# A rotary embedding on one core: VectorE's program aligned to an instruction-fetch line, and ScalarE's copies by half rows

## The chip, the cores and the metric

The kernel runs on one core of one Trainium2 chip. The metric is the device time of one execution in microseconds (us). A core has TensorE (PE in the profile), VectorE (DVE), ScalarE (ACT), GpSimd (POOL) and SyncE (SP), which run their own programs and meet at semaphores, and 16 DMA engines between the memory of the chip (HBM) and the on-chip memory, where the tiles lie.

## The reference

The input x has 16 batches of 512 positions of 1,024 numbers (16 heads of 64). In each head the first 32 numbers are rotated against the last 32, by tables of cosines and sines that depend on the position. All is float32.

```python
x1, x2 = x[..., :half_dim], x[..., half_dim:]
rotated = np.concatenate([x1 * cos - x2 * sin, x1 * sin + x2 * cos], axis=-1)
```

So each number is multiplied by a cosine, and the number 32 places away in its head, multiplied by plus or minus the sine, is added. Input and output have 33.55 MB each.

## The kernel before, in words

Two batches make a tile of 128 partitions by 8 rows of 1,024 numbers (4 MiB); there are eight tiles, in five buffers. SyncE issues all transfers from one queue: the first tile in two parts with the sine and cosine tables between them, the next four tiles, four tiny reads into a spare buffer (L92), and then the stores, one per tile, but two of 2 MiB for the last. Loads of tiles 5 to 7 follow the third store (L78, L74).

Before the tiles, GpSimd writes an identity matrix. VectorE clears a tile of zeros (L97), with which TensorE opens its PSUM buffers (L101), and copies the identity twice beside itself (L109, `spread`). TensorE multiplies the tables by it (L113, L114), which lays them out over all partitions; VectorE writes signed sines from that (L116, L117, L119).

The eight rows of a tile are computed in three ways:

- Six rows, as three pairs (`PAIRS`): VectorE multiplies by the cosine into PSUM (L141, `pd`), GpSimd multiplies the swapped halves by the sine (L165, `b`), VectorE adds the two back into the tile (L189).
- Row 3 (`pe_half`), in two halves of 512: VectorE's cosine product goes into `pe_ps` (L141), GpSimd makes the sine product, TensorE adds it through the identity (L176), and ScalarE copies the sum back into the tile (L181).
- Row 0, the own row: VectorE multiplies by the cosine into `own_ps` (L141), then by the sine in place (L150). TensorE adds the swapped row to `own_ps` through the identity, 512 numbers at a time, which are the two halves of `own_ps` (L176), and ScalarE copies the sum back (L209).

The order of the work is written out by hand and stands in the loop over the tiles; nothing reorders it. The cosine product of the next tile's own row comes near the end of each tile's turn.

Of the kernel before, what the change touches and what calls it, by code (L numbers as in the profile page):

```python
# [28 lines left out]
def kernel(  # L29
# [13 lines left out]
    nc = tc.nc  # L43
# [20 lines left out]
    pd = ctx.enter_context(tc.tile_pool(name="pd", bufs=1, space=bass.MemoryType.PSUM))  # L64

    ctx.enter_context(tc.manual_schedule())

    tiles = [None] * NT

# [28 lines left out]
    own_ps = pe.tile([P, dim], FP32)  # L98
    pe_ps = pe.tile([P, BANK], FP32)
    for ps in (own_ps[:, :BANK], own_ps[:, BANK:], pe_ps):  # L100
# [9 lines left out]
        out=spread.rearrange("p (b q) -> p b q", b=NB),  # L110
        in_=bass.AP(tensor=eye.tensor, offset=eye.offset, ap=[eye.ap[0], [0, NB], [1, PB]]),
# [12 lines left out]
    def swapped(r):  # L124
        n = r.shape[1] // hd
        return bass.AP(tensor=r.tensor, offset=r.offset + half, ap=[r.ap[0], [hd, n], [-half, 2], [1, half]])

    def rows(t, k, n=1):
        return tiles[t][:, k * dim : (k + n) * dim]

    def cos_product(out, r, k, n=1):

        c = cos_t[:, k * half : (k + n) * half]
        m = r.shape[1] // (n * half)
        if n == 1:
            cb = bass.AP(tensor=c.tensor, offset=c.offset, ap=[c.ap[0], [0, m], [1, half]])
            o, i = (z.rearrange("p (a j) -> p a j", j=half) for z in (out, r))
        else:
            cb = bass.AP(tensor=c.tensor, offset=c.offset, ap=[c.ap[0], [half, n], [0, m], [1, half]])
            o, i = (z.rearrange("p (k a j) -> p k a j", k=n, j=half) for z in (out, r))  # L140
        nc.vector.tensor_tensor(out=o, in0=i, in1=cb, op=ALU.mult)  # L141

    def own_product(r):

        s = bass.AP(
            tensor=own_t.tensor,
            offset=own_t.offset + half,
            ap=[own_t.ap[0], [0, nh], [-half, 2], [1, half]],
        )
        nc.vector.tensor_tensor(out=heads(r), in0=heads(r), in1=s, op=ALU.mult)  # L150
# [16 lines left out]
    def sin_rows(t, k, n):  # L167
        b = bp.tile([P, 2 * dim], FP32, name="b")[:, : n * dim]
        sin_product(b, rows(t, k, n), k, n)
        return b  # L170

    def parts(r):
        return [r[:, i * BANK : (i + 1) * BANK] for i in range(r.shape[1] // BANK)]

    def pe_add(ps, other):
        nc.tensor.matmul(out=ps, lhsT=ident, rhs=other, start=False, stop=True, skip_group_check=True)  # L176

    def pe_half(k, r, b):
        cos_product(pe_ps, r, k)
        pe_add(pe_ps, b)  # L180
        nc.scalar.copy(out=r, in_=pe_ps)  # L181

    def pair_product(t, k):
        ps = pd.tile([P, 2 * dim], FP32, name="pd")
        cos_product(ps, rows(t, k, 2), k, 2)
        return ps, rows(t, k, 2)

    def pair_sum(ps, r, b):
        nc.vector.tensor_tensor(out=r, in0=ps, in1=b, op=ALU.add)  # L189

    def stores(t):
        lo = 0
        for hi in LAST_OUT if t == NT - 1 else (KK,):
            store(t, lo, hi)
            lo = hi
        if t + 1 == NT - BUFS:
            for n in range(BUFS, NT):
                load(n)

    cos_product(own_ps, rows(0, ROW_OWN), ROW_OWN)  # L200
    for t in range(NT):
        first, second, third = PAIRS
        b1 = sin_rows(t, first[0], 2)
        p1 = pair_product(t, first[0])
        r0 = rows(t, ROW_OWN)
        own_product(r0)
        for ps, r in zip(parts(own_ps), parts(r0)):
            pe_add(ps, swapped(r))
        nc.scalar.copy(out=r0, in_=own_ps)  # L209
        b3 = sin_rows(t, ROW_PE, 1)  # L210
        b2 = sin_rows(t, second[0], 2)
        pair_sum(*p1, b1)
        h0, h1 = zip(parts(rows(t, ROW_PE)), parts(b3))
        pe_half(ROW_PE, *h0)
        p2 = pair_product(t, second[0])
        b1 = sin_rows(t, third[0], 2)
        pair_sum(*p2, b2)
        pe_half(ROW_PE, *h1)
        p1 = pair_product(t, third[0])
        if t + 1 < NT:  # L220
            cos_product(own_ps, rows(t + 1, ROW_OWN), ROW_OWN)
        pair_sum(*p1, b1)
        stores(t)
# [35 lines left out]
```

## Time and profile before

| | |
|---|---|
| median of 7 runs | 162.65 us (162.2 to 162.82) |
| the profiled execution | 162.36 us |
| its span, first to last instruction | 160.6 us (160.57) |
| busy: VectorE, GpSimd, TensorE, ScalarE | 136.2, 127.2, 56.9, 18.7 us |
| DMA: data packets, share of 16 engines | 98.0% |
| DMA: instruction packets | 1 |

The span is what the profile draws; the rest of an execution's time lies before and after it. Busy times are sums over one engine's instructions. The DMA share is the time that packets took, out of 16 engines over the whole span. An instruction packet is a piece of an engine's program that is fetched while it runs. In lists of groups, a row names line, engine, operation, what it writes and reads, and how often; then its busy time, the mean of one in ns, and the idle time before it with what ended it. In the table of stretches, the columns are TensorE's matmuls and weight loads, VectorE, ScalarE and GpSimd with their busy time and number of instructions, then TensorE's granted clock, the DMA share and GB/s. In a timeline, the first two numbers are start and length.

### The profile page before, as it was taken

The page shows a single profiled execution, that of the slowest core. Times are in us where ns is not written, and L with a number is a line of the kernel's source. Part 1 is how long each engine was busy: PE and PEld are TensorE (multiplying, and loading weights), DVE is VectorE, ACT ScalarE, POOL GpSimd, SP SyncE. Part 2 cuts the span into 40 slices and gives each one's busy share as a digit, 9 for nine tenths or more (in the row PEclk, how much of TensorE's full clock was granted, in tenths as well). Part 3 has the DMA queues.
Part 4 walks back from the last instruction along what each step waited for, and adds up shares of the span by engine and source line. Part 5 has one row for each costly group of instructions (what it writes and reads, how often), then busy time and mean ns, then how long its engine had stood idle before and what let it go on. Part 6 is the DMA issues. An engine that isn't in the chain of part 4 may idle for free.

```text
span 160.6 us, 443 instructions
## 1 busy us (share of the span) xinstructions
PE 56.9 (35%) x71; PEld 18.3 (11%) x71; DVE 136.2 (85%) x85; ACT 18.7 (12%) x25; POOL 127.2 (79%) x38
## 2 busy tenths in 40 slices
PE   3041905057303930193108420672049201930000
PEld 0011201021002200130003000210022001300000
DVE  1059969999999999999999999999999999999000
ACT  0001411003100211012100310031002200211000
POOL 1039999999999999988998899898998899840000
PEclk9999975556855595558555765568555955585555
DMA  5999999999999999999999999999999999999994
GB/s 187 396 413 473 392 490 424 392 465 449 392 433 474 400 400 506 400 392 514 402 392 465 441 400 433 473 392 424 473 408 424 473 408 408 482 416 400 429 424 192
DMA packets 2787, 67.25 MB, mean 419 GB/s; under 512 B 354, under 2 KB 482, under 8 KB 482
## 3 DMA queue, kind: packets, MB, share of 16 engines
q1 hardware_dynamic: 2786, 67.24, 98.0%
q14 instruction: 1, 0.01, 0.0%
HBM read 33.69 MB, written 33.55 MB: 419 GB/s over the span
## 4 chain that ended last, share of the span: by engine, by line
DVE 68%; issue 12%; POOL 6%; DMA 4%; PE 1%; SPq 0%; DVEq 0%
DVE xt L189 33%; DVE pd L141 31%; POOL b L165 6%; DMA b<-in_sin_dram 4%; DVE pe_ps L141 3%; PE tab L113 1%; PE tab L114 1%; DVE sns L116 0%; DVE xt L150 0%; DVE own_ps L141 0%; SPq L74 0%; DVE sns L117 0%; DVEq L189 0%
## 5 line engine op out<-in xcount | busy, mean ns | idle before, releaser
L165 POOL TENSOR_TENSOR b<-xt,sns 128x2048 f32<-128x2048 f32 (+1 forms) x32 | 126.5, 3980 | 14.7 <-DVE sns L117 9.3
L189 DVE TENSOR_TENSOR xt<-pd,b 128x2048 f32<-128x2048 f32 x24 | 54.9, 2286 | 2.4 <-POOL b L165 1.6
L141 DVE TENSOR_TENSOR pd<-xt,tab 128x2048 f32<-128x2048 f32 x24 | 55.0, 2291 | 0.2
L176 PE MATMUL own_ps<-xt,ident 128*128 128x512 f32 x32 | 30.0, 1093 | 59.1 <-DVE xt L150 53.3
L176 PE MATMUL pe_ps<-b,ident 128*128 128x512 f32 x32 | 25.0, 874 | 22.7 <-DVE pe_ps L141 22.7
L176 PEld LDWEIGHTS own_ps<-xt,ident 128*128 128x128 f32 x32 | 9.4, 324 | 75.2 <-DVE xt L150 60.5
L209 ACT COPY xt<-own_ps 128x1024 f32<-128x1024 f32 x8 | 8.1, 1012 | 78.1 <-PE own_ps L176 78.1
L181 ACT COPY xt<-pe_ps 128x512 f32<-128x512 f32 x16 | 9.4, 586 | 33.2 <-PE pe_ps L176 33.2
L176 PEld LDWEIGHTS pe_ps<-b,ident 128*128 128x128 f32 x32 | 7.4, 253 | 43.0 <-DVE pe_ps L141 34.5
L141 DVE TENSOR_TENSOR pe_ps<-xt,tab 128x512 f32<-128x512 f32 x16 | 11.0, 686 | 0.0
L141 DVE TENSOR_TENSOR own_ps<-xt,tab 128x1024 f32<-128x1024 f32 x8 | 9.8, 1224 | 0.0
L150 DVE TENSOR_TENSOR xt<-xt,tab 128x1024 f32<-128x1024 f32 x8 | 9.7, 1214 | 0.0
L116 DVE TENSOR_SCALAR sns<-tab 128x256 f32<-128x256 f32 x1 | 0.4, 425 | 8.2 <-PE tab L114 8.2
L209 ACT ACT_TABLE_LOAD x1 | 1.3, 1283 | 15.4 <-DVE xt L150 15.4
L113 PE MATMUL tab<-b,spread 64*128 64x256 f32 x2 | 1.2, 696 | 5.0 <-DMA b<-in_sin_dram 5.0
L101 PE MATMUL own_ps<-zero 128*128 128x512 bf16 x2 | 1.0, 620 | 1.2 <-DVE zero L97 1.2
L113 PEld LDWEIGHTS tab<-b,spread 64*128 64x128 f32 x2 | 0.5, 307 | 5.9 <-issue 5.9
L114 PE MATMUL tab<-b,spread 64*128 64x256 f32 x2 | 1.1, 631 | 0.0
L97 DVE MEMSET zero<- 128x256 uint32 x1 | 0.3, 272 | 0.9 <-PEq L240 0.9
L114 PEld LDWEIGHTS tab<-b,spread 64*128 64x128 f32 x2 | 0.7, 333 | 0.2
L101 PE MATMUL pe_ps<-zero 128*128 128x512 bf16 x1 | 0.6, 634 | 0.0
L101 PEld LDWEIGHTS <-zero 128*128 128x128 bf16 x3 | 0.3, 123 | 1.5 <-DVE zero L97 1.2
(9 smaller groups left out, 1.8 us busy)
## 6 DMA issues: line engine op xcount, KB each, us to landing
xt<-in_x_dram SPq DMA_DIRECT2D x7, 4096.0 KB, 29.7
out_dram<-xt SPq DMA_DIRECT2D x7, 4096.0 KB, 24.7
out_dram<-xt SPq DMA_DIRECT2D x2, 2048.0 KB, 10.4
xt<-in_x_dram SPq DMA_DIRECT2D x1, 2560.0 KB
xt<-in_x_dram SPq DMA_DIRECT2D x1, 1536.0 KB
b<-in_sin_dram SPq DMA_DIRECT2D x1, 64.0 KB
b<-in_cos_dram SPq DMA_DIRECT2D x1, 64.0 KB
spare<-in_sin_dram SPq DMA_DIRECT2D x1, 0.1 KB
```

Of the source, the lines that this page charges most:

```text
L97: nc.vector.memset(zero, 0.0)
L101: nc.tensor.matmul(out=ps, lhsT=zero[:, :P], rhs=zero, start=True, stop=True)
L113: nc.tensor.matmul(out=sin_t, lhsT=spread, rhs=sin_sb, start=True, stop=True)
L114: nc.tensor.matmul(out=cos_t, lhsT=spread, rhs=cos_sb, start=True, stop=True)
L116: nc.vector.tensor_scalar_mul(out=sns[:, :, 0, :], in0=sin_k, scalar1=-1.0)
L141: nc.vector.tensor_tensor(out=o, in0=i, in1=cb, op=ALU.mult)
L150: nc.vector.tensor_tensor(out=heads(r), in0=heads(r), in1=s, op=ALU.mult)
L165: nc.gpsimd.tensor_tensor(out=o, in0=i, in1=sb, op=ALU.mult)
L176: nc.tensor.matmul(out=ps, lhsT=ident, rhs=other, start=False, stop=True, skip_group_check=True)
L181: nc.scalar.copy(out=r, in_=pe_ps)
L189: nc.vector.tensor_tensor(out=r, in0=ps, in1=b, op=ALU.add)
L209: nc.scalar.copy(out=r0, in_=own_ps)
```

## The change

```diff
     ctx.enter_context(tc.manual_schedule())
+    nc.vector.addr_align(128, max_nops=0)
...
         own_product(r0)
         for ps, r in zip(parts(own_ps), parts(r0)):
             pe_add(ps, swapped(r))
-        nc.scalar.copy(out=r0, in_=own_ps)
+            nc.scalar.copy(out=r, in_=ps)
```

The first line puts an alignment into VectorE's program, ahead of its first instruction of the kernel's body: what follows it begins at a multiple of 128 instruction slots, and VectorE gets there by a branch over the padding. The second moves ScalarE's copy of the own row into the loop over its halves. In the built program ScalarE has 16 copies of 512 numbers where there were eight of 1,024; TensorE's instructions are the same and in the same order, but the matmul of the second half waits for a semaphore of ScalarE that it didn't wait for before, and VectorE's cosine product into `own_ps` no longer waits for TensorE. ScalarE's program grows from 45 to 53 instructions; VectorE's goes from 125 to 122, with the alignment itself among them. GpSimd's and SyncE's are as they were.

## The prediction

> **What bounds the kernel now.** I read four views, in this order. First the page's slices, the DMA table and the chain of the work that ended last:
>
> ```profile
> span 160.6 us, 443 instructions
> ...
> DMA  5999999999999999999999999999999999999994
> ...
> q1 hardware_dynamic: 2786, 67.24, 98.0%
> q14 instruction: 1, 0.01, 0.0%
> ...
> DVE 68%; issue 12%; POOL 6%; DMA 4%; PE 1%; SPq 0%; DVEq 0%
> ```
>
> The chain blames VectorE (68%), but the 16 DMA engines are busy from the first slice to the last, and only one packet is not data: one instruction fetch. Two rows that can't both bind, so the second view is the table of stretches:
>
> ```profile
> 124.00:141.00 17.00, 6.64 (x9) 2.10 (x8) 16.86 (x11) 2.18 (x3) 15.86 (x5) 0.60 1.00 432
> 141.00:149.00 8.00, 1.32 (x3) 0.30 (x2) 7.14 (x4) 1.17 (x2) 1.46 (x1) 0.71 0.98 424
> 149.00:161.00 12.00, 0.00 (x0) 0.00 (x0) 0.00 (x0) 0.00 (x0) 0.00 (x0) 0.50 0.78 332
> ```
>
> After 149 us no engine computes, and the DMA engines still have nearly 10 us of work (0.78 x 12 = 9.4 us). Who is late at the end is therefore a question of backlog. Third, the sync queue:
>
> ```profile
> 0.73 0.38 SPq L74 DMA_DIRECT2D xt<-in_x_dram  x1
> ...
> 145.48 3.13 SPq L78 DMA_DIRECT2D out_dram<-xt  x2
> ```
>
> The last two stores (2 MiB each) are issued at 145.48 and 148.28 us (148.28 from the issue's own record), and in the packet records their first 16 KiB packets start at 148.53 and about 153.4 us, each just where the transfer before it ends. From issue to first packet an idle engine takes 1.02 us (0.73 to 1.75 at the start). So the stores are early by 148.53 - 145.48 - 1.02 = 2.0 us and 153.4 - 148.28 - 1.02 = 4.1 us. The bound is the DMA engines: full packets of 32 KiB take 1.21 us at the median and 1.21 us at the least, so there is no slack inside them; VectorE has about 2 us in hand at the end.
>
> The fourth view is the packets one DMA engine at a time. Each transfer ends with 16 four-byte completion writes, one per DMA engine; the spread of their times shows which engine lags. At 71.1 us the last engine is 0.27 us behind the median; at 80.7 us it is 0.65; at the end 0.84, with the second 0.56 behind and the third 0.29. Between the two first figures, at 79.69 us, the page's one instruction packet runs: 8,192 bytes, 309 ns, and the 32 KiB packet next to it in time took 472 ns longer than its fellows. The lag rises by 0.648 - 0.267 = 0.38 us and never shrinks: this fetch fell on the DMA engine that was last already, and the program ends when that engine ends (159.40 us; SyncE goes on at 159.75; span 160.57).
>
> [...]
>
> **Part one: the alignment.** Whose fetch is it? The span holds 123 VectorE records, 94 + 71 of TensorE, 62 of GpSimd, 50 of SyncE and 43 of ScalarE. The fetch comes 0.68 us after VectorE starts its 65th (79.00 us, a sum of L189); the 66th starts at 81.32 us, right after the 65th, so nothing stalled. If every engine has about as many instructions before the span, a boundary at VectorE's 65th leaves the shorter programs with none. TensorE should then cross too and shows no fetch[...]; a boundary of TensorE's (at its 90th) or GpSimd's (36th) would have VectorE cross there too, earlier, and no such fetch is shown. I take it as VectorE's (three in four).
>
> With the change, the instruction after the branch is slot 0 of a line. VectorE's built program goes from 125 to 122 instructions, the alignment included: some 118 follow it, fewer than 128. So the crossing moves from 79.7 us to the branch, about 0.7 us. Removed: one fetch from the last DMA engine, 0.38 us there. The gain at the end is smaller if another engine then ends last: the second is at 0.56, so 0.84 - 0.56 = 0.29 us. Where the second engine's lag doesn't recur, the whole 0.38 counts. I take the middle, 0.33 us.
>
> Added: the branch, and perhaps a wait for its line. Not in this trace; bounds: 0, if the line is there, to about 1.0 us (from VectorE's 65th at 79.00 to the end of the fetch at 79.995)[...]. What hides it:
>
> ```profile
> 0.86 0.27 DVE L97 MEMSET zero<- 128x256 uint32 x1 [0.86 <-PEq L240]
> ...
> 2.01 0.63 PE L101 MATMUL pe_ps<-zero 128*128 128x512 bf16 x1
> ...
> 7.69 1.19 PE L113 MATMUL tab<-b,spread 64*128 64x256 f32 x2 [5.04 <-DMA b<-in_sin_dram]
> 9.77 0.42 DVE L116 TENSOR_SCALAR sns<-tab 128x256 f32<-128x256 f32 x1 [8.21 <-PE tab L114]
> ```
>
> Behind the branch stand the zero fill, TensorE's three matmuls on it and the spread copy; TensorE then waits until 7.69 us for the sine table, 5.0 us of cover. I cost it at nothing; without cover it would be its own length. SyncE's first load isn't behind it, and data packets start only at 1.75 us, so a fetch at 0.8 to 1.7 us finds idle DMA engines.
>
> **Part two: copies by half rows.** Eight copies of 1,012 ns become 16 of 586 ns (the L181 row, same form): 16 x 0.586 - 8 x 1.012 = +1.28 us of ScalarE, which is idle 88% of the span. The order of issue on TensorE is unchanged, but its second own-row matmul now waits for the copy of the first half. In the tile at 34 us:
>
> ```profile
> 33.87 3.78 PE L176 MATMUL own_ps<-xt,ident 128*128 128x512 f32 x4 [6.90 <-DVE xt L150]
> ...
> 37.45 1.87 PE L176 MATMUL pe_ps<-b,ident 128*128 128x512 f32 x2
> 37.69 1.01 ACT L209 COPY xt<-own_ps 128x1024 f32<-128x1024 f32 x1 [10.09 <-PE own_ps L176]
> 38.93 2.29 DVE L189 TENSOR_TENSOR xt<-pd,b 128x2048 f32<-128x2048 f32 x1
> 39.36 0.59 ACT L181 COPY xt<-pe_ps 128x512 f32<-128x512 f32 x1 [0.66 <-PE pe_ps L176]
> 41.13 0.69 DVE L141 TENSOR_TENSOR pe_ps<-xt,tab 128x512 f32<-128x512 f32 x1
> ```
>
> The second matmul starts at 35.74 now. Its predecessor's two passes end at 35.95, plus 0.04 to ScalarE, 0.59 of copy, 0.05 back: 36.63, so it is late by 0.9 us[...]. Queued behind it on TensorE is the pe_ps matmul; its copy ends at 39.94 + 0.9 = 40.84 instead of 39.94. VectorE's next product into pe_ps waits for that copy and starts at 41.13: 0.2 to 0.3 us remain. So nothing on VectorE, and if the cover falls short by, say, 0.1 us, seven tiles lose 0.7 us out of the 2.0 in hand. The second pe_ps row of the last tile (copy done at 145.46, the store right after) lies 4 us behind the own row and doesn't move. No DMA is added or moved; SyncE's order is the same.
>
> **Sum.** Profiled execution 162.36 = span 160.57 + 1.79 outside. Span: -0.33 (ends 0.29 and 0.38) + 0 + 0 = 160.24; with the 1.79, 162.03. The profiled run lay 0.29 below the median of 162.65; against the median I say 162.65 - 0.33 = 162.32, about 162.3.
>
> **Rivals.**
> *The fetch stays* (it is another engine's, or the next line is still fetched under full load). For: the owner is inferred; if a fetch is triggered by position in a line, a program begun at slot 0 may ask for its next line half-way. Against: the count of records above. Time 162.65.
> *The closing code crosses the line* (the slower side). Some 118 of 128 slots are used, and what follows at the end would lie in the next line; if that is fetched only when reached, the cost is about the 1.0 us from above, after the last store, hidden by nothing: 162.65 + 1.0 - 0.33 = 163.3. It decides only if the closing code within the timed stretch goes past slot 127, and no copy of the next line came earlier. For: 1.79 us lie outside the span. Against: the 66th instruction waited for nothing when its line was crossed[...].
> *ScalarE's handshake delays VectorE.* It needs a delay d with 7 x (d - 1.1) > 2.0 us, that is d over 1.4 us, against the 0.7 to 0.9 worked out; at d = 1.6 the loss is 3.5 - 2.0 = 1.5 us: 163.8 with the gain.
>
> **How the numbers follow.** My forecast (the fetch leaves the loaded stretch) has 0.60, the staying fetch 0.25, the closing code 0.10, the handshake 0.05. A difference of 0.2% (0.33 us) is about what a measurement of this kernel can tell from none. The forecast's gain of 0.29 to 0.38 straddles that: 0.43 of its 0.60 faster, 0.15 same, 0.02 slower. The staying fetch: 0.19 same, 0.03 either side. The other two: slower, 0.02 of them same. Together faster 0.46, same 0.36, slower 0.18. Range 161.9 (the 0.38, and most of the 0.45 between the median and the fastest of the runs shown) to 162.95 (no gain, plus the spread of the runs above, and part of the closing code); the forecast's own is 161.95 to 162.6.
>
> **What would show it.** Right: no instruction packet in the loaded stretch, or one near 1 us; the last DMA engine's completion 0.3 us earlier against the median of the 16; the spread copy later but L116 still near 9.8; L209 with 16 copies near 586 ns; VectorE's groups and its period of 16.97 us per tile as before. Wrong: an instruction packet still near 80 us, L141 waiting on ScalarE, or a longer stretch outside the span.

## The result, and the profile after

The changed kernel is slower by 0.5%: 163.36 us median (162.88 to 164.22, 14 runs) against 162.58 (162.2 to 162.98, 33 runs), a ratio of 1.0052 with a 95% interval of 1.004 to 1.0064. That is 0.78 us more where the prediction had 0.33 us less. The profiled execution took 163.68 us with a span of 161.88, so 1.80 us lie outside the span, as before (1.79). The 1.31 us that this execution's span is longer are all inside.

The page of the changed kernel, with the same rows as were shown of the kernel before:

```profile
span 161.9 us, 448 instructions
...
DMA  5999999999999999999999999998999999999991
...
q1 hardware_dynamic: 2786, 67.24, 97.2%
q14 instruction: 2, 0.01, 0.0%
...
DVE 65%; issue 14%; POOL 6%; DMA 4%; PE 1%; SPq 0%; DVEq 0%
```

The data are the same, but the last digit of the DMA row is 1 where it was 4: in the last slice hardly any of the 16 DMA engines works. The second "instruction" packet in the count is one of 40 bytes from the start of the program; the one of 8,192 bytes is what matters. In the packet records it now runs at 3.42 us, and none runs near 80 us.

The table of stretches of the changed kernel (columns as before: TensorE, its weight loads, VectorE, ScalarE, GpSimd, granted clock, DMA share, GB/s):

```profile
124.00:141.00 17.00, 6.74 (x9) 1.97 (x8) 16.86 (x11) 2.34 (x4) 15.86 (x5) 0.60 1.00 432
141.00:149.00 8.00, 3.03 (x5) 0.64 (x3) 7.79 (x5) 1.75 (x3) 2.30 (x1) 0.71 0.98 422
149.00:161.90 12.90, 0.00 (x0) 0.00 (x0) 0.09 (x1) 0.00 (x0) 0.00 (x0) 0.50 0.73 312
```

VectorE's busy time in a tile's 17 us is what it was, 16.86 us, and until 149 us the DMA engines are as full. After that they have the same work (0.73 x 12.9 = 9.4 us) but take longer for it, because one of them is behind. The beginning, in order of time:

```profile
0.73 0.38 SPq L75 DMA_DIRECT2D xt<-in_x_dram  x1
...
1.40 0.27 DVE L98 MEMSET zero<- 128x256 uint32 x1 [1.40 <-PEq L241]
1.58 0.15 DVE L110 COPY spread<-ident 64x128 f32<-64x128 f32 x1
...
2.55 0.63 PE L102 MATMUL pe_ps<-zero 128*128 128x512 bf16 x1
...
8.55 1.19 PE L114 MATMUL tab<-b,spread 64*128 64x256 f32 x2 [5.36 <-DMA b<-in_sin_dram]
...
10.62 0.43 DVE L117 TENSOR_SCALAR sns<-tab 128x256 f32<-128x256 f32 x1 [8.89 <-PE tab L115]
```

VectorE starts 0.54 us later (1.40 instead of 0.86), which TensorE's wait for the sine table covers, as foreseen. But the table itself is 0.86 us late (8.55 instead of 7.69). Of the 48 completion writes of the first three transfers, the sine table's among them, the last three come at 7.55, 7.72 and 7.90 us, where before the last came at 6.98: one DMA engine is late with the first loads. So all tiles begin 0.85 us later. The last two stores follow, and still they are early:

```profile
146.32 3.13 SPq L79 DMA_DIRECT2D out_dram<-xt  x2
```

The 16 completion writes of each transfer show the rest. One engine is 1.06 us behind the median of the 16 already at 12.9 us (before: 0.31), 1.58 at 61.5 us, and 2.12 at 109.9 us and at the end (before: 0.84). 2.12 - 0.84 = 1.28 of the 1.31 us: in this execution the time is lost on one DMA engine.

### The profile page after: what moved, and what is told of

Same layout as the page of the kernel before. It is cut to its first block, busy times and chain, and to the rows that moved or that the text cites. A ratio compares the mean times of both kernels' runs of the same rounds, so it can differ in the third digit from the quotient of the medians.

```text
span 161.9 us, 448 instructions
## 1 busy us (share of the span) xinstructions
PE 59.9 (37%) x71; PEld 17.6 (11%) x71; DVE 136.1 (84%) x85; ACT 20.0 (12%) x33; POOL 127.1 (79%) x38
## 3 DMA queue, kind: packets, MB, share of 16 engines
q1 hardware_dynamic: 2786, 67.24, 97.2%
## 4 chain that ended last, share of the span: by engine, by line
DVE 65%; issue 14%; POOL 6%; DMA 4%; PE 1%; SPq 0%; DVEq 0%
DVE xt L190 33%; DVE pd L142 26%; POOL b L166 6%; DVE pe_ps L142 6%; DMA b<-in_sin_dram 4%; PE tab L114 1%; PE tab L115 1%; DVE xt L151 0%; DVE sns L117 0%; DVE own_ps L142 0%; SPq L75 0%; DVE sns L118 0%; DVEq L190 0%
## 5 line engine op out<-in xcount | busy, mean ns | idle before, releaser
L177 PE MATMUL own_ps<-xt,ident 128*128 128x512 f32 x32 | 33.2, 1139 | 64.1 <-DVE xt L151 52.8
L190 DVE TENSOR_TENSOR xt<-pd,b 128x2048 f32<-128x2048 f32 x24 | 54.9, 2285 | 2.4 <-POOL b L166 1.6
L210 ACT COPY xt<-own_ps 128x512 f32<-128x512 f32 x16 | 9.4, 585 | 89.5 <-PE own_ps L177 89.5
L177 PEld LDWEIGHTS own_ps<-xt,ident 128*128 128x128 f32 x32 | 8.0, 311 | 84.9 <-DVE xt L151 60.3
L177 PEld LDWEIGHTS pe_ps<-b,ident 128*128 128x128 f32 x32 | 8.2, 277 | 33.9 <-DVE pe_ps L142 25.7
L117 DVE TENSOR_SCALAR sns<-tab 128x256 f32<-128x256 f32 x1 | 0.4, 426 | 8.9 <-PE tab L115 8.9
```

What stands on the lines that cost most here:

```text
L117: nc.vector.tensor_scalar_mul(out=sns[:, :, 0, :], in0=sin_k, scalar1=-1.0)
L210: nc.scalar.copy(out=r, in_=ps)
```

## The experiments

**Alignment or half rows?** The first two runs do one part each.

```diff
-            nc.scalar.copy(out=r, in_=ps)
+        nc.scalar.copy(out=r0, in_=own_ps)      # alignment alone: the changed kernel with whole rows
```

> The alignment alone, ScalarE's copy of whole rows as before. Fetch theory (the alignment puts an instruction fetch at 3.4 us among the first loads, on the DMA engine that ends last): an instruction packet near 3.4 us, sine tables late, L116 near 10.6 us instead of 9.77, time as the changed kernel, 163.2 to 163.5 us. Half-row theory (TensorE's wait for ScalarE costs the time): 162.6 us.

Measured: 164.55 us, ratio 1.0113 (1.0091 to 1.0136): slower than with both parts. The fetch is at 3.42 us, L117 at 10.72 us. The last slice of this kernel's DMA row is empty but for one engine:

```profile
span 162.5 us, 444 instructions
...
DMA  5999998998999998998999999999989989989990
```

The spans of its six runs (161.3 to 162.7) are not far from those of the changed kernel (161.1 to 162.4), but 2.2 to 2.6 us lie outside them, instead of 1.8. The packet records show a second fetch at 164.79 us, after the span's end. That fits closing code that runs past the end of a fetched piece of the program; of that more below.

```diff
-    nc.vector.addr_align(128, max_nops=0)        # half rows alone: the changed kernel without the alignment
```

> The half-row copies alone, no alignment. Fetch theory: no packet near 3.4 us; VectorE's program lacks a semaphore instruction per tile from the second tile on, so the one fetch moves a few instructions later than the 65th, to some 82 to 88 us; time as before, 162.4 to 162.8 us. Half-row theory: 163.2 to 163.5 us.

Measured: 163.0 us, ratio 1.0024 (1.0012 to 1.0036). The fetch moves to 82.33 us, from 79.69. Only VectorE's program was shortened, so a later fetch fits VectorE's; but 62 of its records start before the fetch now, where 65 did, so the packet does not simply follow one record by a fixed time. That the fetch is VectorE's is shown by the runs below, in which it goes wherever VectorE's alignment goes. The small loss was not expected. It is not the handshake between ScalarE and TensorE: VectorE's last sum starts at 145.80 us, before at 145.96. The fetch now falls among loads 5 to 7 instead of the end of the stores before them, and the last engine's lag goes from 0.39 to 0.96 us (before: 0.27 to 0.65), then to 1.36 at 109.9 us (before: 0.84).

**Where the fetch falls.**

```diff
-    nc.vector.addr_align(128, max_nops=0)
...
+    nc.vector.addr_align(128, max_nops=0)        # just ahead of the first own-row product
     cos_product(own_ps, rows(0, ROW_OWN), ROW_OWN)
```

> The changed kernel with the alignment moved behind the table copies, just ahead of VectorE's first product into own_ps (9.8 us). Fetch theory: the packet comes about 2 us after that, at 11 to 13 us, when the first loads are long under way; L116 at 9.8 us again; if a fetch costs about 0.4 us wherever the data packets are in step, time 162.5 to 162.8; if a fetch on this DMA engine always costs 0.75 us, 163.0 to 163.4. Late-start theory (the 0.85 us by which VectorE and GpSimd begin later is what reaches the end): 162.6.

Measured: 163.93 us, ratio 1.0071 (1.0052 to 1.009), above what either theory gave, though the tables are in time again. The timeline of VectorE in this kernel:

```profile
9.62 0.42 DVE L116 TENSOR_SCALAR sns<-tab 128x256 f32<-128x256 f32 x1 [8.07 <-PE tab L114]
9.97 0.41 DVE L117 COPY sns<-tab 128x256 f32<-128x256 f32 x1
10.41 0.23 DVE L119 COPY tab<-sns 128x64 f32<-128x64 f32 x1
11.06 1.23 DVE L141 TENSOR_TENSOR own_ps<-xt,tab 128x1024 f32<-128x1024 f32 x1 [0.42 <-DVE tab L119]
```

L116 starts at 9.62 us, earlier than in the kernel before, and the end is later than in the changed kernel. So the late start isn't the cause. The fetch runs at 14.01 us; the lag rises there from 0.30 to 0.86 us, and then again without any fetch: 0.85 to 1.26 between 42 and 61 us, 1.23 to 2.30 at 109.9. These are the two places where the queue goes over from loads to stores. That gave the switch theory, tried below: a DMA engine that is late at such a place comes out of it later still.

```diff
     nc.vector.tensor_scalar_mul(out=sns[:, :, 0, :], in0=sin_k, scalar1=-1.0)
+    idle = fixed.tile([P, 768], FP32)
+    nc.vector.memset(idle, 0.0)                  # the kernel before, with a late start
     nc.vector.tensor_copy(out=sns[:, :, 1, :], in_=sin_k)
```

> The kernel before, with an extra fill of 128x768 on VectorE between the two signed-sine instructions, so that VectorE and GpSimd start the tiles about 0.8 us later, with no fetch at 3.4 us. Late-start theory: 163.3 to 163.5 us. Fetch theory: the stores are early by 2 us, so nothing, 162.5 to 162.8 us.

Measured: 162.86 us, ratio 1.0009 (0.9999 to 1.0019). The own-row product starts at 11.71 us, 0.89 later than before and as in the changed kernel (11.68). A late start of that size costs at most 0.2%, not 0.5%.

```diff
     for t in range(NT):
         first, second, third = PAIRS
+        if t == 3:
+            nc.vector.addr_align(128, max_nops=0)   # instead of ahead of the body
```

> The changed kernel with the alignment moved to the start of tile 3's turn (about 64 us), so that the fetch comes at 66 to 69 us, in the stretch of stores, past the switch from loads to stores at 51.8 us. Switch theory (a DMA engine that lags has its last reads slowed while the other 15 already write, so an early fetch is paid again at the switches at 51.8 and 109.9 us): no jump of the lag at 51.8, about 0.4 us from the fetch, some 0.1 to 0.5 at 109.9; final lag 0.8 to 1.4 us; time 162.6 to 163.1, below the 163.4 of the changed kernel. Plain-branch theory (the branch itself costs): 163.3 to 163.6.

Measured: 162.33 us, ratio 0.9996 (0.9982 to 1.0009): the whole loss is gone, with the same branch, the same half rows and the same number of fetches. The page of this kernel:

```profile
span 160.4 us, 448 instructions
...
DMA  5999999999999999999999999999999999999994
...
q1 hardware_dynamic: 2786, 67.24, 98.1%
q14 instruction: 1, 0.01, 0.0%
```

The last digit of the DMA row is 4 again. The fetch is at 65.24 us, among stores; the lag goes from 0.30 to 0.59 us, doesn't rise at 109.9, and is 0.59 at the end. The expectation was 0.8 to 1.4, so the run is better than the theory's numbers. In VectorE's timeline the branch, at 60.84 us in the records, leaves no gap: it lies under the product that starts at 60.62 and runs for 1.22 us, and the sum follows at once:

```profile
60.62 1.22 DVE L141 TENSOR_TENSOR own_ps<-xt,tab 128x1024 f32<-128x1024 f32 x1
61.76 2.28 DVE L189 TENSOR_TENSOR xt<-pd,b 128x2048 f32<-128x2048 f32 x1
64.07 2.29 DVE L141 TENSOR_TENSOR pd<-xt,tab 128x2048 f32<-128x2048 f32 x1
```

The next run is the same with `t == 2`, one tile earlier.

> The changed kernel with the alignment at the start of tile 2's turn (about 44 us), one tile earlier than in the run at tile 3, so that the fetch comes at 46 to 49 us, among the loads. Switch theory (a fetch among loads costs its DMA engine 0.55 us or more, and an engine that lags by over about 0.7 us at a switch from loads to stores lags more after it): a lag of about 0.9 us before the switch at 51.8, more after it, 1.5 to 2.7 at the end; time 163.0 to 163.9. If only a fetch in the first few us hurts: 162.3 to 162.6 as with the alignment at tile 3.

Measured: 162.84 us, ratio 1.0028 (1.0018 to 1.0039). The fetch is at 48.18 us, the last of the loads before the switch; the lag is 0.44 us before it, 0.82 at 61.7 us, 1.24 after 109.9. The time is just under the lower end that was given, and clear of the kernel before: 17 us of place decide over 0.5 us.

```profile
span 161.0 us, 448 instructions
...
DMA  5999999999999999999999999999999999999993
```

**Lag without a fetch.**

```diff
+    extra = fixed.tile([1, 4096], FP32)
+    nc.sync.dma_start(out=extra, in_=x_v[0][:1, :4096])   # the kernel before, one more row
     for t in range(1, BUFS):
         load(t)
```

> The kernel before, with one extra read of a single row of 16 KiB into a spare buffer among the first loads: 0.61 us of work for one DMA engine and no fetch at 3.4 us. Switch theory: that engine lags by 0.6 to 0.9 us from 13 us on, by 0.4 to 0.5 more after 51.8 us, and by 0.5 to 1.4 more after 109.9 us, as if a fetch had been there; time 163.2 to 163.9. Additive theory (a lag stays as it was made): at most 0.6 us at the end, on another engine than the fetch at 80 us, so 162.6 to 162.9. Fetch-only theory (fetches do something that data doesn't): 162.6 to 162.9.

Measured: 162.49 us, ratio 1.0004 (0.999 to 1.0019). This speaks against the switch theory as it was put: I had given a lag of 0.6 to 0.9. But the row made a lag of only 0.47 us (a packet of 16 KiB takes 0.61 in the kernel before), presumably since it fell on an engine that wasn't behind, and the lag rose to 0.61 at the first switch and from 0.68 to 0.71 at the second. Either small lags do not grow, or lags from data don't; this run alone can't tell.

**What makes the lag jump.** Without the four tiny reads (L92):

```diff
-    for i, n in enumerate(EXTRA):
-        nc.sync.dma_start(out=spare[:n, i], in_=sin_v[:n, :16])   # the changed kernel without them
```

> The changed kernel without the four tiny reads into the spare buffer, whose packets run at 51.8 us. Switch theory: the jump of the lag by about 0.5 us at 51.8 stays. If the tiny reads on the lagging DMA engine make it, it goes away, and the time falls to about 162.9.

Measured: 163.95 us (five runs), ratio 1.0077 (1.0051 to 1.0104). In the profiled run the lag stays at 0.85 us through 51.8 us, and rises from 0.84 to 1.33 at 109.9. But that was the fastest of the five (163.15 us), and the others, without packet records, were 0.7 to 1.0 us slower. So the tiny reads may make the first jump, and a late engine does not jump at every switch; as an account of the time the run is inconclusive.

```diff
-        if t + 1 == NT - BUFS:
-            for n in range(BUFS, NT):
-                load(n)
+        if t == 1:
+            load(BUFS)
+            load(BUFS + 1)
+        if t == 3:
+            load(BUFS + 2)
```

> The changed kernel with loads 5 and 6 behind store 1, and load 7 behind store 3, so that loads give way to stores at about 51.8, 90.5 and 119.5 us and no longer at 109.9. Switch theory: the last engine's lag rises at 51.8, near 90 and near 119 us, and not at 109.9. Clock-of-its-own theory (something at 51, 80 and 109 us whatever the transfers do): rises at 109 us again. Time, if no store or load comes late, 163.3 to 164.5.

Measured: 164.31 us, ratio 1.0102 (1.0075 to 1.0129). The lag rises from 1.18 to 1.62 us at 51.8 and from 1.60 to 2.48 at 90.0, where a single 32 KiB packet, the last load before the stores, took 0.88 us longer than its fellows. At 109.9, where all other runs with a lag over 0.75 us have their jump, nothing happens (2.48 to 2.53). The late jump thus moves with the switch and does not keep its place in time. At the third switch near 119 us the lag went from 2.53 to 2.40; there the expected rise did not come. The time isn't comparable, since the whole order is another.

**The closing code.**

```diff
-            nc.vector.addr_align(128, max_nops=0)
+            nc.vector.addr_align(128, offset=51, max_nops=0)   # at tile 3's turn
```

> The alignment at tile 3's turn, to slot 51 of a line instead of slot 0, so that VectorE's last instructions of the span stand at about slots 120 to 123 and its closing code crosses into the next line, as it seems to with the alignment alone. The fetch at 65 us stays. Closing-code theory: the span as with the alignment at tile 3 (160.4 us), the stretch outside the span 2.4 us instead of 1.8, time 162.9 to 163.1. Otherwise 162.3 to 162.5.

Measured: 162.59 us, ratio 1.0009 (1.0001 to 1.0017), with 1.7 to 1.8 us outside the span in all 15 runs. By the expectation's count of slots the closing code should have crossed, and nothing outside the span shows that it did; why is open. The other way to the same count is four fills at the end of the changed kernel:

```diff
+    pads = fixed.tile([16, 64], FP32)
+    for i in range(4):
+        nc.vector.memset(pads[:, i * 16 : (i + 1) * 16], 0.0)
```

> The changed kernel, half rows and early alignment, with four tiny fills at the end of VectorE's program, so that 122 instructions of the program follow the alignment, as with the alignment alone, instead of 118. The fills run when VectorE has nothing left to do. Closing-code theory: the stretch outside the span grows from 1.8 to 2.2 to 2.6 us as it did there, with an instruction packet about 2 us after the span's end, the span stays 161.1 to 162.4, time 163.8 to 164.1 us. If it was the whole rows and not the number of instructions: outside 1.8, time 163.4.

Measured: 164.3 us, ratio 1.0106 (1.0086 to 1.0126); the spans of its six runs are 161.2 to 162.4, and 2.2 to 2.6 us lie outside. A fetch runs at 164.66 us. The time is just above what the theory gave. So 122 instructions after the alignment at the start cost what 118 don't, whole rows or half rows, and 0.4 to 0.8 us of that lie outside the span.

```diff
+        if t == 3:
+            nc.vector.addr_align(128, max_nops=0)   # the kernel before, whole rows
```

> The kernel before with the alignment at tile 3's turn, and ScalarE's copies of whole rows. Switch theory: the half rows do nothing but shorten VectorE's program, and with the fetch at 65 us both are as fast, 162.2 to 162.5. If the half rows themselves gain or cost, the difference to the run with half rows and the alignment at tile 3 (162.33) shows it.

Measured: 162.53 us, ratio 1.0012 (0.9999 to 1.0026), beside 162.33 with half rows. The two intervals overlap; the half rows cost nothing that can be seen here. The fetch is at 65.26 us, the lag goes from 0.36 to 0.73 and, at 109.9, from 0.77 to 0.98.

No variant beats the kernel before beyond its interval.

**All runs side by side.** Lag of the last DMA engine behind the median of the 16, in us, from the completion writes of the profiled run (one execution per kernel):

| run | fetch at | 42 us | 61 us | 100 us | after 109.9 |
|---|---|---|---|---|---|
| alignment at tile 3, half rows | 65.2 | 0.18 | 0.30 | 0.65 | 0.59 |
| extra row | 79.8 | 0.46 | 0.61 | 0.68 | 0.71 |
| before | 79.7 | 0.31 | 0.28 | 0.70 | 0.84 |
| alignment at tile 3, whole rows | 65.3 | 0.13 | 0.36 | 0.77 | 0.98 |
| alignment at tile 3, slot 51 | 65.4 | 0.34 | 0.56 | 0.79 | 1.20 |
| alignment at tile 2 | 48.2 | 0.44 | 0.82 | 0.82 | 1.24 |
| late start | 80.0 | 0.27 | 0.21 | 0.84 | 1.37 |
| no tiny reads | 3.2 | 0.85 | 0.86 | 0.84 | 1.33 |
| half rows alone | 82.3 | 0.29 | 0.33 | 0.97 | 1.36 |
| alignment ahead of the product | 14.0 | 0.85 | 1.26 | 1.23 | 2.30 |
| changed kernel | 3.4 | 1.07 | 1.58 | 1.55 | 2.12 |
| alignment alone | 3.4 | 1.18 | 1.63 | 1.58 | 2.74 |
| four fills | 3.8 | 1.26 | 1.65 | 1.65 | 2.71 |

At 109.9 us a lag up to 0.70 us gains at most 0.14, one of 0.77 to 0.97 gains 0.2 to 0.5, one over 1.2 gains 0.6 to 1.2. The extra row's small lag is in line with that, whatever made it. In all 13 kernels the span less the lag at the end is 159.7 to 160.0 us, so the last DMA engine accounts for the differences between these spans.

## Why the prediction was wrong, point by point

*What bounds the kernel* was right: the DMA engines (97.2% of the span with data), and of these the last. The stores were 0.84 us later than before and lost nothing; the late start alone gave 1.0009.

*Whose fetch it is* was right: with the alignment moved within VectorE's program the fetch came at 3.42, 14.01, 48.18 and 65.24 us, and none near 80 us any more. That a line holds 128 instructions, as the forecast counted, is not shown: the packet's 8,192 bytes are measured, and how many instructions they hold is in no trace. Nor is it shown why TensorE has no fetch.

*Where the fetch goes* is the step that failed: "a fetch at 0.8 to 1.7 us finds idle DMA engines". The branch itself is at 0.76 us in the records, as predicted, but the packet runs 2.67 us after it, at 3.42 us, 1.7 us after the first data packet. The 1.0 us that I had taken for the way from a crossing to the end of its fetch was read from VectorE's last start before the packet, which need not be the crossing. Measured from a branch that the trace shows, the fetch comes 2.67, 3.58 (alignment ahead of the product), 4.02 (tile 2) and 4.39 us later (tile 3). By these delays, an estimate, the crossing in the kernel before lay at 75.3 to 77.0 us and not at 79.0. Moreover what the branch goes to seems to have been there already, since VectorE works on at 1.40 us, 2 us before the packet. What is fetched at 3.42 us is then presumably a line after it, of which, by the same count, the span would run nothing; that is not shown. In any case the change takes a fetch out of the middle and puts one into the start.

*The price of a fetch* was wrong as well. I had 0.38 us, once, as read at 79.7 us among the last of the stores. At nearly the same place (80.0 us) the kernel with the late start shows a rise of 0.63 us. Of the fetches at 65 us, among stores, the first lag measured after them was 0.16 to 0.37 us larger; at 14.0 and 82.3 us, among loads, 0.55 and 0.57; with a fetch in the first 4 us the lag at 42 us is 0.85 to 1.26, against 0.13 to 0.46 in the kernels whose fetch comes after 42 us. These are lags of whichever engine is last, and the fetch can fall on another. In the run at slot 51 the two last engines were 0.56 and 0.21 us behind before the fetch, and 0.72 and 0.56 after it, which is most simply read as a rise of about 0.5 us on one that was not last. So these figures do not set stores clearly apart from loads; the early fetches do stand out. And a lag doesn't only "never shrink": at 109.9 us one of 0.77 us or more grew, in every run of the table. The rival *the fetch stays* had the packet under full load at 162.65 us, as neutral. It should have had the worse price: after an early fetch both switches are still to come.

*The half rows.* The forecast of nothing was right for VectorE, but by a hair. In the tile at 35 us of the changed kernel:

```profile
34.72 2.08 PE L177 MATMUL own_ps<-xt,ident 128*128 128x512 f32 x2 [7.60 <-DVE xt L151]
36.78 0.69 DVE L142 TENSOR_TENSOR pe_ps<-xt,tab 128x512 f32<-128x512 f32 x1
36.83 0.58 ACT L210 COPY xt<-own_ps 128x512 f32<-128x512 f32 x1 [9.10 <-PE own_ps L177]
...
37.47 2.07 PE L177 MATMUL own_ps<-xt,ident 128*128 128x512 f32 x2 [0.68 <-ACT xt L210]
...
41.29 0.58 ACT L182 COPY xt<-pe_ps 128x512 f32<-128x512 f32 x1 [1.12 <-PE pe_ps L177]
41.98 0.69 DVE L142 TENSOR_TENSOR pe_ps<-xt,tab 128x512 f32<-128x512 f32 x1
```

The second matmul waits 0.68 us for the copy, and ScalarE's copy of pe_ps ends at 41.87, 0.11 us before VectorE's product needs it, instead of the 0.2 to 0.3 worked out. The sum L190 starts at 34.58 us in tile 1 and at 136.41 us in tile 7, six periods of 16.97 us, so VectorE lost nothing. What I overlooked is what the half rows do in the built program: they take four instructions out of VectorE's program, which seems to keep the closing code within its line (1.80 us outside the span, and no fetch after it). Beside the alignment they are worth 0.6% (ratios 1.0113 and 1.0052), about 1.0 us. Four fills put back in their place cost nearly all of that again (1.0106), so it is the instructions and not the size of the copies; 0.4 to 0.8 us of it lie outside the span, and the rest, inside, is not explained.

*The closing code* was the rival on the slower side. In the changed kernel it did not happen (1.80 us outside the span). With four instructions more it seems to, by the fetch at 164.66 us, and at 0.4 to 0.8 us instead of the 1.0 given.

*What stays open*: why the last loads of a late engine are slow while the others store (in the changed kernel one 32 KiB packet at 109.2 us took 1.82 us, where 1.21 is the median), and why not at every switch; why the tiny reads seem to matter at 51.8 us; whether the fetch always falls on the same DMA engine, since the records don't name it; and why the program at slot 51 showed no crossing. Every kernel here has one such fetch within its span, so the 0.33 us that taking it out was to gain were never put to the test.

## What to carry to other kernels

Here the DMA engines were full from start to end (98.0% before, 97.2% after), and the time was that of the one engine that ended last. In such a kernel, look at the spread of the completions of each transfer, not only at the mean share. A piece of work that stayed in every variant, as the instruction fetch did here, can have a price that depends on where it falls: in this kernel, moving it from 79.7 to 65.2 us changed nothing that could be measured, and moving it among the first loads, to 3.4 us, cost 0.5%. When an instruction is moved to act earlier, take the delay to what it triggers from an event that the trace shows, not from the nearest one before it.

## What the runs showed of the hardware that was not expected

- After the branch of the alignment, VectorE's next instruction came 0.56 to 0.66 us later where nothing else was running on it (0.76 to 1.40 us in the changed kernel, 10.43 to 10.99 with the alignment ahead of the product), with no fetch packet in between. Under a product of 1.22 us (tile 3) it cost VectorE nothing.
- In these runs the 8,192-byte fetch started 2.5 to 4.4 us after the branch that seems to trigger it. Among full packets it took 309 to 333 ns itself, and the 32 KiB packet that started as it ended took 0.35 to 0.66 us longer than the usual 1.21 (in the kernel before: 309 ns, and 1.69 us).
- A DMA engine that was behind by 0.77 us or more when the others went over from loads to stores at 109.9 us fell 0.2 to 1.2 us further behind. It is no rule for every switch: without the tiny reads a lag of 0.85 us stayed as it was at 51.8 us, and in the run with the other order one of 2.53 us did not grow near 119 us. In that run one packet of 32 KiB took 2.09 us instead of 1.21.
- With 122 instead of 118 instructions after the alignment at the start, 2.2 to 2.6 us lie outside the span instead of 1.8. At tile 3 a count of slots that should have crossed too left it at 1.8.
